# A decoder trunk on one core: the second FFN product in seven block products, with block sums made in DRAM

## The chip, the core and the metric

One core of a Trainium2 chip runs the whole program. TensorE (PE) multiplies into PSUM; VectorE (DVE), ScalarE (ACT) and GpSimd (POOL) work elementwise; SyncE's queue (SP) issues the loads and stores. The metric is the device time in microseconds of one execution: the median of three runs before the change is 1895.09 us (1895.04 to 1895.27).

## The reference

Two layers, each of three sub-layers with a residual and a layer norm: a token mixer (a gated recurrence beside windowed attention with learned sinks), cross-attention into 256 memory tokens, and a gated FFN. 512 tokens of width 1024, all float32. The change concerns the second product of the FFN, `... @ wo`, whose weight has 2816 rows and 1024 columns:

```python
D_FF = -(-8 * D_MODEL // (3 * 256)) * 256          # 2816

def swiglu(u, wi, wo):
    gate, up = jnp.split(u @ wi, 2, axis=-1)
    return (jax.nn.silu(gate) * up) @ wo

for l in range(DEPTH):                             # DEPTH = 2
    ...
    h = layer_norm(DEEPNORM_ALPHA * h + swiglu(h, ffn_wi[l], ffn_wo[l]), ln3_g[l], ln3_b[l])
```

and, of the attention, the maximum over the scores and the sink of each head:

```python
    sink = sinks.astype(jnp.float32).reshape(N_KV_HEADS, GROUP)[None, None, :, :, None, None]
    sink = jnp.broadcast_to(sink, scores.shape[:-1] + (1,))
    probs = jax.nn.softmax(jnp.concatenate([scores, sink], axis=-1), axis=-1)[..., :-1]
```

## The kernel before

Every float32 operand is split into a high part, rounded for fast multiplication, and a low part. A product of tiles is three matmuls: high by high, high by low, low by high. A weight comes as 128x1024 tiles of 512 KB. The class `Weights` keeps one list of them for the whole program, in order of use: `dma` loads the next into one of four `raw` buffers, on SP's queue; `split` makes the high part `whi` on ACT (L122) and the low part `wlo` on DVE (L123), and asks for further loads. `next` hands out a tile and splits `la` tiles ahead. The first product of the FFN and the query product of the cross-attention already work in seven block products (`split_quad`, `proj_pair`): there sums of weight blocks are made on DVE.

In the second product of the FFN, `out_norm` walks over the 22 row tiles of `wo`. For each row tile and each of four groups of 128 tokens it does six matmuls of 128x512 into two PSUM banks, so that eight banks hold the whole result; the activations `hs` are split by `h_parts` (ACT L271, DVE L272). The last five row tiles are taken group by group, and `norm` reads the residual x and the banks (L421, L435). Before these five, x is loaded back from `x_keep` in DRAM (L505).

The windowed attention (`swa_s`) works in 32 units a layer. A unit multiplies queries and keys, and builds the masked scores in a tile `sm` that has one more column for the sink. GpSimd copies the sink into that column (L603); ACT (L604) and DVE (L606) write the scores; DVE reduces the maximum over both (L608); the exponentials follow on ACT. There are six `sm` buffers. Before the change these 64 copies, some constants and six additions in the last norm are all that GpSimd has in its queue.

The code says which engine does what. A scheduler then orders the instructions of each engine, earlier code first among those that it reckons ready; each engine takes its queue in that order, and an instruction waits at its head on semaphores. The instructions of PE, DVE and ACT stand nearly as the code has them.

Of the kernel before, what the change touches and what calls it, by code (L numbers as in the profile page):

```python
# [7 lines left out]
F32 = mybir.dt.float32  # L8
# [37 lines left out]
class Weights:  # L46
# [27 lines left out]
    def rows(self, w, c0, n):  # L74
        for k in range(n):
            self.specs.append([(w[k * P:(k + 1) * P, c0:c0 + D], lambda t: t)])

    def gates(self, a, b):
        for n in range(4):
            self.specs.append([  # L80
                (m[n].rearrange("(k p) c -> p k c", p=P),
                 lambda t, i=i: t[:, i * 512:(i + 1) * 512].rearrange("p (k c) -> p k c", k=2))
                for i, m in enumerate((a, b))])
# [22 lines left out]
    def split(self):  # L106
        j = self.n_split
        if j >= len(self.specs):
            return
        while self.n_dma <= j:  # L110
            self.dma()
        if j in self.quad:
            self.drain()
            self.gen = self.split_quad(j)
            self.drain()
            return
        self.n_split += 1
# [95 lines left out]
class Trunk:  # L213
    def __init__(self, ctx, tc, a):
        self.tc = tc
        self.nc = tc.nc
        self.a = a
        self.L = a["w_in"].shape[0]
        pool = lambda name, bufs, **kw: ctx.enter_context(tc.tile_pool(name=name, bufs=bufs, **kw))
        self.const = pool("const", 1)  # L220
        self.pg = pool("pg", N_PAGES)
        self.raw = pool("raw", N_RAW)
        self.hpool = pool("hp", 8)
        self.smp = pool("sm", 3)
        self.sml = pool("sml", 8)
        self.psp = pool("ps", 8, space=PSUM)
        self.W = Weights(self)
        self.now = 0.0
        self.pend = []

    def page(self, dt=F32, name="pg"):
# [235 lines left out]
                nc.sync.dma_start(out=self.x_dram[t * P:(t + 1) * P, :], in_=xt)  # L467

    def out_norm(self, act, nk, res, gv, bv, last=False, prefetch=0, between=None,
                 want_T=False, restore=False, spread=0.0):  # L470

        nc = self.nc
        g = self.page(F32, "ln_g")
        nc.sync.dma_start(out=g, in_=gv.partition_broadcast(P))
        b = self.page(F32, "ln_b")
        nc.sync.dma_start(out=b, in_=bv.partition_broadcast(P))
        acc = [[self.ps("acc") for _ in range(2)] for _ in range(NT)]
        self.x_done = [False] * NT
        self.want_T, self.spread = want_T, spread
        self.Bf = {}  # L480

        cut = last

        def step(k, t, w, parts=((0, S), (S, D))):
            ah, al = act(k)
            hi, lo = w
            cs = slice(t * P, (t + 1) * P)
            kw = {"skip_group_check": True} if parts[0][1] - parts[0][0] < S else {}
            out = lambda c0, c1: acc[t][c0 // S][:, c0 % S:c0 % S + c1 - c0]
            for c0, c1 in parts:  # L490
                self.mm(out(c0, c1), ah[:, cs], hi[:, c0:c1], k == 0, False, **kw)
# [165 lines left out]
    def schedule_weights(self):  # L657
        a, W = self.a, self.W
        for l in range(self.L):
            wi = a["w_in"][l]  # L660
            XR, GR, QC, KV, GN, GA = 0, 1024, 2048, 3072, 3328, 4352
            W.cols(wi, KV, 1)
            W.cols(wi, QC, 1)
            W.cols(wi, KV + P, 1)
            W.cols(wi, QC + P, 1)
            W.cols(wi, GA, 1)
            for j in range(8):
                if j < 6:
# [12 lines left out]
            W.rows(a["ckv_w"][l], D, 8)  # L681
            for h in range(4):
                W.quads(a["cq_w"][l], 2 * h * P, (2 * h + 1) * P)
            W.rows(a["co_w"][l], 0, 8)
            for m in range(2):
                W.cols(a["ffn_wi"][l], m * P)
                W.cols(a["ffn_wi"][l], DFF + m * P)
            for m in range(2, NF):
                W.quads(a["ffn_wi"][l], m * P, DFF + m * P)
            W.rows(a["ffn_wo"][l], 0, NF)  # L690

    def layer_params(self, l):
        nc, a = self.nc, self.a
# [316 lines left out]
    def ffn(self, l, last):  # L1010
        nc, a, W = self.nc, self.a, self.W
        W.la = 0
        H, hs = {}, {}

        def act(m, g, u0, u1):
            s = self.half(name="silu")
            nc.scalar.activation(out=s, in_=g, func=AF.Silu)
            if m % 2 == 0:
                pg = self.page(F32, "h")
                H[m], H[m + 1] = pg[:, :S], pg[:, S:]  # L1020
            if u1 is None:
                nc.vector.tensor_tensor(out=H[m], in0=s, in1=u0, op=ALU.mult)
            else:
                nc.vector.tensor_tensor(out=H[m][:, :256], in0=s[:, :256], in1=u0, op=ALU.mult)
                nc.vector.tensor_tensor(out=H[m][:, 256:], in0=s[:, 256:], in1=u1, op=ALU.mult)

        def h_parts(k):
            for q in range(k, min(k + 3, NF)):
                if q in H:
                    t = self.page(F32R, "hs")  # L1030
                    self.split_to(t[:, :S], t[:, S:], H.pop(q), scale=1.0 / ALPHA)
                    hs[q] = t
            t = hs[k]
            if k - 1 in hs and k < NF - R3:
                hs.pop(k - 1)
            return t[:, :S], t[:, S:]

        p = self.proj_halves(4)
        act(0, p[0], p[1], None)
        act(1, p[2], p[3], None)  # L1040
        self.xt = [None] * NT
        for m in range(2, NF):
            act(m, *self.proj_pair())
        W.la = 2
        self.T = {}
# [27 lines left out]
    def run(self):  # L1073
        nc, a = self.nc, self.a
        self.xt = [self.page(F32, "x") for _ in range(NT)]
        self.mT_dram = [self.tc.dram_tile([P, 2, 2, MEM], F32, name="mT_keep%d" % i) for i in range(4)]
        self.x_dram = self.tc.dram_tile([S, D], F32, name="x_keep")
        self.xT = self.const.tile([P, ND, 2, S], F32R, name="xT")
        self.ident = self.const.tile([P, P], F32, name="ident")
# [76 lines left out]
```

## Time and profile before

| what | value |
|---|---|
| median of three runs | 1895.09 us |
| the profiled execution | 1894.67 us |
| its span, first to last instruction | 1892.8 us |
| PE busy | 1877.0 us, 99% |
| DVE busy | 1355.4 us, 72% |
| ACT busy | 1010.8 us, 53% |
| GpSimd busy | 27.5 us, 1% |
| moved by DMA | 217.63 MB |

The shares are means over stages of different kinds. The program runs the mixer, the cross-attention and the FFN of layer 0 until 945 us, and those of layer 1 after that. The granted clock of PE is 1.00 in the stages shown.

### The profile page before, as it was taken

What the parts mean: (1) busy time and instruction counts of PE and PEld (TensorE: products, weight loads), DVE (VectorE), ACT (ScalarE), POOL (GpSimd) and SP (SyncE); (2) the same over time, 40 slices, a digit from 0 to 9 for tenths busy, and PEclk for the clock granted to TensorE, in tenths of its full rate; (3) what the DMA queues carried; (4) which work ended last, traced back from release to release, by engine and by line L of the source; (5) the groups of instructions that cost most, each with busy time, mean ns of one, the idle gap of its engine ahead of it and who ended that gap; (6) DMA issues with size and microseconds to landing.
All of it is one profiled execution on the core that took longest, in us unless ns stands there. A gap on an engine that the chain in (4) does not pass through costs nothing.

```text
span 1892.8 us, 28893 instructions
## 1 busy us (share of the span) xinstructions
PE 1877.0 (99%) x11201; PEld 1666.6 (88%) x11201; DVE 1355.4 (72%) x2403; ACT 1010.8 (53%) x1973; POOL 27.5 (1%) x74
## 2 busy tenths in 40 slices
PE   9999999999999999999999999999999999999998
PEld 9888888889998999988898888888899899999886
DVE  6997367559766988873489964675588579888634
ACT  5675167336664655652346742763367556565521
POOL 0000000000000000000000000000000000000001
PEclk9999999999999999999999999999999999999999
DMA  6434133355444333364213441333652523333531
GB/s 183 112 101 121 47 100 90 100 167 191 122 142 127 90 112 101 101 191 144 67 46 104 109 123 44 101 95 95 200 178 80 181 75 112 101 107 107 188 100 45
DMA packets 277753, 217.63 MB, mean 115 GB/s; under 512 B 7792, under 2 KB 254064, under 8 KB 277616
## 3 DMA queue, kind: packets, MB, share of 16 engines
q1 hardware_dynamic: 277616, 215.79, 38.3%
q8 instruction: 88, 1.44, 0.3%
q14 instruction: 49, 0.40, 0.1%
HBM read 196.89 MB, written 12.58 MB: 111 GB/s over the span
## 4 chain that ended last, share of the span: by engine, by line
PE 96%; DVE 3%; ACT 1%; issue 0%; DVEq 0%; ACTq 0%
PE ps L244 40%; PE q L244 25%; PE acc L244 22%; PE cv L244 2%; PE sc L244 2%; PE av L244 1%; PE cs L244 1%; PE pt L248 1%; DVE Bf L346 1%; PE pT L248 1%; PE cT L248 0%; DVE wlo L123 0%; DVE xT L269 0%; DVE T1l L269 0%; PE scr L1062 0%
## 5 line engine op out<-in xcount | busy, mean ns | idle before, releaser
L244 PE MATMUL ps<-xT,whi 128*128 128x512 f32 (+1 forms) x1728 | 478.7, 365 | 1.2 <-ACT xT L268 0.7
L123 DVE TENSOR_TENSOR wlo<-raw,whi 128x1024 fp32r<-128x1024 f32 x239 | 290.4, 1222 | 142.2 <-ACT whi L122 114.0
L244 PEld LDWEIGHTS ps<-xT,whi 128*128 128x128 f32 x1728 | 297.4, 188 | 46.1 <-ACT xT L268 1.5
L122 ACT ACTIVATE whi<-raw 128x1024 fp32r<-128x1024 f32 x239 | 249.4, 1053 | 135.3 <-PE acc L244 52.4
L244 PE MATMUL ps<-xT,wlo 128*128 128x512 f32 (+1 forms) x864 | 310.8, 362 | 0.0
L244 PE MATMUL acc<-whi,hs 128*128 128x512 f32 (+1 forms) x714 | 218.3, 387 | 0.5 <-ACT hs L271 0.5
L244 PEld LDWEIGHTS ps<-xT,wlo 128*128 128x128 f32 x864 | 162.0, 188 | 27.6 <-DVE wlo L123 0.2
L244 PEld LDWEIGHTS acc<-whi,hs 128*128 128x128 f32 x714 | 133.5, 188 | 28.0 <-ACT hs L271 0.9
L244 PE MATMUL q<-xT,wq 128*128 128x256 f32 x1152 | 155.0, 281 | 0.1
L244 PEld LDWEIGHTS q<-xT,wq 128*128 128x128 f32 x1152 | 144.4, 189 | 0.6 <-DVE wq L269 0.5
L377 ACT ACTIVATE c<-q 128x256 f32<-128x256 f32 x192 | 73.5, 383 | 121.7 <-PE q L244 120.9
L244 PE MATMUL acc<-wlo,hs 128*128 128x512 f32 (+1 forms) x357 | 137.9, 386 | 0.0
L269 DVE TENSOR_TENSOR wql<-s,wqh 128x512 fp32r<-128x512 f32 x192 | 128.7, 684 | 1.4 <-ACT wqh L268 1.2
L268 ACT ACTIVATE wqh<-s 128x512 fp32r<-128x512 f32 x192 | 114.8, 622 | 15.2 <-DVE s L152 12.6
L269 DVE TENSOR_TENSOR wq<-raw,wq 128x512 fp32r<-128x512 f32 x144 | 98.4, 683 | 0.0
L268 ACT ACTIVATE wq<-raw 128x512 fp32r<-128x512 f32 x144 | 89.6, 622 | 3.3 <-DMA raw<-in_cq_w_dram 3.3
L244 PE MATMUL acc<-whi,mg 128*128 128x512 f32 x256 | 80.6, 392 | 0.0
L244 PE MATMUL acc<-whi,cO 128*128 128x512 f32 x256 | 80.2, 391 | 0.0
L244 PE MATMUL ps<-ya,whi 128*128 128x512 f32 x256 | 78.9, 389 | 0.0
L244 PEld LDWEIGHTS acc<-wlo,hs 128*128 128x128 f32 x357 | 67.0, 188 | 13.4
L244 PE MATMUL ps<-yr,whi 128*128 128x512 f32 x256 | 78.9, 389 | 0.0
L244 PE MATMUL q<-T4h,wq 128*128 128x256 f32 x384 | 76.7, 282 | 0.0
(237 smaller groups left out, 3968.3 us busy)
## 6 DMA issues: line engine op xcount, KB each, us to landing
raw<-in_ffn_wi_dram SPq DMA_DIRECT2D x88, 512.0 KB, 3.9
raw<-in_w_in_dram SPq DMA_DIRECT2D x84, 512.0 KB, 3.9
raw<-in_ffn_wo_dram SPq DMA_DIRECT2D x44, 512.0 KB, 4.2
raw<-in_ckv_w_dram SPq DMA_DIRECT2D x32, 512.0 KB, 4.5
raw<-in_w_br_attn_dram SPq DMA_DIRECT2D x16, 512.0 KB, 3.9
raw<-in_w_br_rnn_dram SPq DMA_DIRECT2D x16, 512.0 KB, 4.2
raw<-in_w_out_dram SPq DMA_DIRECT2D x16, 512.0 KB, 3.8
x_keep<-y SPq DMA_DIRECT2D x16, 512.0 KB, 2.6
```

The source lines that it names most:

```text
L122: nc.scalar.activation(out=hi, in_=raw, func=AF.Copy)
L123: nc.vector.tensor_sub(out=lo, in0=raw, in1=f(hi))
L244: self.nc.tensor.matmul(out, lhsT=lhsT, rhs=rhs, start=start, stop=stop, **kw)
L248: self.nc.tensor.transpose(out, in_, self.ident)
L268: nc.scalar.activation(out=hi, in_=src, func=AF.Copy)
L269: nc.vector.tensor_sub(out=lo, in0=src, in1=f(hi))
L346: nc.vector.tensor_tensor(out=o, in0=x, in1=y, op=ALU.subtract)
L377: cp = lambda out, in_: nc.scalar.activation(out=out, in_=in_, func=AF.Copy)
```

## The change

The first 2048 of the 2816 rows of `wo` are taken as two by two blocks of 1024 rows and 512 columns, B11, B12, B21 and B22, and the tokens as two halves of 256. The products of halves and blocks, eight of them, are replaced by seven products of sums. Every product has four tiles of 256 rows, and a tile twelve matmuls of 128x512.

The sums of weight blocks, `t[0]` = B11 + B12, `t[2]` = B12 + B22, `t[1]` = t[0] + B22 and `t[3]` = t[1] + B21, are made in DRAM by DMAs on GpSimd's queue: `block_sums` lists 32 of 256x512 for a layer, 16 that copy and 16 that add, and `split` takes one from that list each time. In layer 0 twelve empty entries stand ahead. The sums of activation blocks are made on DVE, in `operand`. Results of products that belong to more than one output block are added to x, or subtracted from it, by DVE out of PSUM (`into_x`); so x is now loaded ahead of the product. `out_norm` goes on in the same banks with the six row tiles that are left.

```diff
+    def blocks(self, w):
+        for j in range(4):
+            self.specs.append([(w[j * 256:(j + 1) * 256, :].rearrange("(k p) c -> p k c", p=P),
+                                lambda t: t.rearrange("p (k c) -> p k c", k=2))])
@@ def split(self):
         if j >= len(self.specs):
             return
+        if self.K.bg:
+            self.K.bg.pop(0)()
@@ def out_norm(..., acc=None, k0=0):
-        acc = [[self.ps("acc") for _ in range(2)] for _ in range(NT)]
+        fresh = [[acc is None or n is None for n in row] for row in acc] if acc else [[True] * 2] * NT
+        acc = [[acc[t][i] if not fresh[t][i] else self.ps("acc") for i in range(2)] for t in range(NT)]
-        for k in range(nk - res):
+        for k in range(k0, nk - res):
@@ def schedule_weights(self):
-            W.rows(a["ffn_wo"][l], 0, NF)
+            wo, t = a["ffn_wo"][l], self.wsum[l]
+            for b in (wo[0:D, 0:S], t[0], t[1], wo[D:2 * D, S:D], t[2], wo[D:2 * D, 0:S], t[3]):
+                W.blocks(b)
+            W.rows(wo[2 * D:DFF, :], 0, NF - 2 * ND)
+    def block_sums(self, l):
+        dma = self.nc.gpsimd.dma_start
+        wo, t = self.a["ffn_wo"][l], self.wsum[l]
+        B11, B12, B21, B22 = (wo[r * D:(r + 1) * D, c * S:(c + 1) * S] for r in range(2) for c in range(2))
+        seq = ((t[0], B11, 0), (t[2], B12, 0), (t[0], B12, 1), (t[2], B22, 1),
+               (t[1], t[0], 0), (t[1], B22, 1), (t[3], t[1], 0), (t[3], B21, 1))
+        for out, in_, add in seq:
+            for j in range(4):
+                r = slice(j * 256, (j + 1) * 256)
+                kw = {"accum_op": ALU.add} if add else {}
+                self.bg.append(lambda o=out[r, :], i=in_[r, :], kw=kw: dma(out=o, in_=i, **kw))
@@ def ffn(self, l, last):
+        W.la = 3
+        self.T = {}
+        self.xt = [self.page(F32, "x") for _ in range(NT)]
+        for t in range(NT):
+            nc.sync.dma_start(out=self.xt[t], in_=self.x_dram[t * P:(t + 1) * P, :])
+        acc = self.wo_seven(Hp)
...
         W.la = 2
         self.out_norm(h_parts, NF, R3, a["ln3_g"][l], a["ln3_b"][l], last=last,
-                      prefetch=0 if last else F3, restore=True)
+                      prefetch=0 if last else F3, acc=acc, k0=2 * ND)
+    def wo_seven(self, Hp):
+        ...
+        def product(p, b, first):
+            for j in range(4):
+                hi, lo = (t.rearrange("p (k c) -> p k c", k=2) for t in W.next())
+                i = p * 4 + j
+                while todo and todo[0][0] * 4 + todo[0][1] <= i + 2:
+                    operand(*todo.pop(0))
+                ah, al = ops.pop((p, j))
+                for k in range(2):
+                    for t in range(2):
+                        c = slice(t * P, (t + 1) * P)
+                        self.mm(b[t], ah[:, k, c], hi[:, k, :], first and j + k == 0, False, **kw)
+                        self.mm(b[t], ah[:, k, c], lo[:, k, :], False, False, **kw)
+                        self.mm(b[t], al[:, k, c], hi[:, k, :], False, j + k == 4, **kw)
+        def into_x(t0, hf, b, op):
+            for t in range(2):
+                x = self.xt[t0 + t][:, hf * S:(hf + 1) * S]
+                tt(out=x, in0=x, in1=b[t], op=op)
+        product(0, b1, True)
+        into_x(0, 0, b1, ALU.add)
+        product(1, b2, True)
+        into_x(2, 1, b2, ALU.add)
+        product(2, b1, False)
+        into_x(0, 1, b1, ALU.subtract)
+        product(3, b2, False)
+        product(4, b1, False)
+        into_x(2, 1, b1, ALU.subtract)
+        product(5, b3, True)
+        product(6, b1, False)
@@ def run(self):
         for l in range(self.L):
+            if l == 0:
+                self.bg = [lambda: None] * 12
+            self.block_sums(l)
             self.mixer(l, prm)
```

Two places show how the order of instructions changes. The first is GpSimd's queue at the start of the program. Before, the copies of the sink `sk` into the score tiles `sm` stand there, the first six of them with no other wait than that for the sink:

```order
L603 COPY sm<-sk 128x2 [waits DMAHW3_49]
L603 COPY sm<-sk 128x2 x5
L603 COPY sm<-sk 128x2 [waits DVE_49,PE_49,Pool_49] x2
L603 COPY sm<-sk 128x2 [waits PE_49,DVE_49,Activation_49,Pool_49] x6
L603 COPY sm<-sk 128x2 [waits DVE_49,PE_49,Pool_49]
```

Now the same queue begins as follows (`wsum_0_86` to `wsum_3_89` are the four sums of layer 0, `wsum_0_90` to `wsum_3_93` those of layer 1; rows that read alike are counted):

```order
L716 DMA wsum_0_86<-in_ffn_wo_dram 256x512 x4
L716 DMA wsum_2_88<-in_ffn_wo_dram 256x512 x4
L716 DMA wsum_0_86<-in_ffn_wo_dram 256x512 x4
L716 DMA wsum_2_88<-in_ffn_wo_dram 256x512 x4
L716 DMA wsum_1_87<-wsum_0_86 16x8192 x4
L716 DMA wsum_1_87<-in_ffn_wo_dram 256x512 x4
L716 DMA wsum_3_89<-wsum_1_87 16x8192 x4
L613 COPY sm<-sk 128x2 x6
L716 DMA wsum_3_89<-in_ffn_wo_dram 256x512 x4
L716 DMA wsum_0_90<-in_ffn_wo_dram 256x512 x4
L716 DMA wsum_2_92<-in_ffn_wo_dram 256x512 x4
```

28 transfers stand ahead of the first six copies. After these come the rest of layer 0's and, following one another, those of layer 1, up to the seventh copy, shown here with the semaphores that each waits for (DMASW0 to DMASW7 count the landings of GpSimd's transfers, eight in turn):

```order
L716 DMA wsum_3_93<-wsum_1_91 16x8192 [waits DMASW4_49]
L716 DMA wsum_3_93<-wsum_1_91 16x8192 [waits DMASW5_49]
L716 DMA wsum_3_93<-wsum_1_91 16x8192 [waits DMASW6_49]
L716 DMA wsum_3_93<-wsum_1_91 16x8192 [waits DMASW7_49]
L716 DMA wsum_3_93<-in_ffn_wo_dram 256x512 [waits DMASW0_49]
L716 DMA wsum_3_93<-in_ffn_wo_dram 256x512 [waits DMASW1_49]
L613 COPY sm<-sk 128x2 [waits DVE_49,PE_49,Pool_49]
```

62 of the 64 transfers stand ahead of the seventh copy. The rows of PE, DVE and ACT in the two mixers are those of before.

The second place is ACT's queue where the second product of the FFN begins in layer 0. Before, a weight split stands ahead of the silu, and the operand's splits right behind it:

```order
L377 ACTIVATE c_8677<-q_8674 128x256 [waits PE_49]
L122 ACTIVATE whi<-raw 128x1024 [waits DMAHW3_49,DVE_49]
L1017 ACTIVATE silu<-gt 128x512 [waits DVE_49]
L271 ACTIVATE hs<-h 128x512 x3
L122 ACTIVATE whi<-raw 128x1024 [waits DMAHW4_49]
```

Now the two weight splits stand between the silu and the first operand `hq`:

```order
L386 ACTIVATE c_8717<-q_8714 128x256 [waits PE_49]
L1043 ACTIVATE silu<-gt 128x512 [waits DVE_49,Activation_49]
L130 ACTIVATE whi<-raw 128x1024 [waits DMAHW3_49]
L130 ACTIVATE whi<-raw 128x1024 [waits DMAHW4_49]
L280 ACTIVATE hq<-h 128x512
```

The operand moved behind one weight split more, and the split that stood ahead of the silu moved behind it.

## Rows read from the trace of the kernel before

**Rows 1.** The page: the span, and busy us of each engine.

```profile
span 1892.8 us, 28893 instructions
...
PE 1877.0 (99%) x11201; PEld 1666.6 (88%) x11201; DVE 1355.4 (72%) x2403; ACT 1010.8 (53%) x1973; POOL 27.5 (1%) x74
```

**Rows 2.** Busy time by stretch: bounds, length, PE, PEld, DVE, ACT, POOL, clock, DMA share, GB/s.

```profile
60.00:100.00 40.00, 40.00 (x223) 34.25 (x223) 39.26 (x109) 26.59 (x78) 3.32 (x11) 1.00 0.35 92
...
826.00:945.00 119.00, 118.73 (x531) 98.26 (x530) 55.63 (x82) 42.87 (x63) 0.00 (x0) 1.00 0.42 129
```

**Rows 3.** Timeline of PE in the second product: start, us, engine, line, operation, count.

```profile
830.38 0.84 PE L244 MATMUL acc<-whi,hs 128*128 128x512 f32 x3
...
831.74 0.84 PE L244 MATMUL acc<-whi,hs 128*128 128x512 f32 x3
```

**Rows 4.** Groups by line and shape, 826 to 910 us: busy, mean ns.

```profile
L123 DVE TENSOR_TENSOR wlo<-raw,whi 128x1024 fp32r<-128x1024 f32 x23 | 28.1, 1223 | 36.6 <-ACT whi L122 21.5 <-issue 8.8 <-PE acc L244 6.4
L122 ACT ACTIVATE whi<-raw 128x1024 fp32r<-128x1024 f32 x22 | 23.0, 1053 | 32.4 <-PE acc L244 28.2 <-DVE hs L272 2.7 <-DMA raw<-in_ffn_wo_dram 1.5
L272 DVE SCALAR_TENSOR_TENSOR hs<-h,hs 128x512 fp32r<-128x512 f32 x19 | 12.9, 686 | 8.9 <-ACT hs L271 8.9
L271 ACT ACTIVATE hs<-h 128x512 fp32r<-128x512 f32 x19 | 11.6, 622 | 18.5 <-PE acc L244 18.5
```

**Rows 5.** Timeline of all engines at the entry of that product.

```profile
824.02 1.05 ACT L122 ACTIVATE whi<-raw 128x1024 fp32r<-128x1024 f32 x1
...
825.38 0.63 ACT L1017 ACTIVATE silu<-gt 128x512 f32<-128x512 f32 x1 [0.30 <-DVE gt L378]
...
825.91 1.66 ACT L271 ACTIVATE hs<-h 128x512 fp32r<-128x512 f32 x3
...
826.58 0.50 PE L244 MATMUL acc<-whi,hs 128*128 128x512 f32 x1 [0.27 <-ACT hs L271]
...
826.76 0.42 DVE L1025 TENSOR_TENSOR h<-silu,c 128x256 f32<-128x256 f32 x1
...
827.09 1.89 DVE L272 SCALAR_TENSOR_TENSOR hs<-h,hs 128x512 fp32r<-128x512 f32 x3
```

**Rows 6.** Timeline of GpSimd: the first seven sink copies.

```profile
21.73 1.80 POOL L603 COPY sm<-sk 128x2 f32<-128x2 f32 x6 [21.29 <-DMA sk<-in_sinks_dram]
49.23 0.29 POOL L603 COPY sm<-sk 128x2 f32<-128x2 f32 x1 [25.71 <-DVE qr L528]
```

**Rows 7.** Timeline of DVE: the first and seventh reduction, a weight split.

```profile
39.00 0.41 DVE L608 TENSOR_REDUCE nm<-sm 128x2 f32<-128x258 f32 x1
...
57.55 1.22 DVE L123 TENSOR_TENSOR wlo<-raw,whi 128x1024 fp32r<-128x1024 f32 x1
58.68 0.41 DVE L269 TENSOR_TENSOR PT<-pT,PT 128x256 fp32r<-128x256 f32 x1
...
60.70 0.42 DVE L608 TENSOR_REDUCE nm<-sm 128x2 f32<-128x258 f32 x1
```

**Rows 8.** Busy time by stretch at the program's start, columns as above.

```profile
0.00:20.00 20.00, 18.08 (x132) 17.55 (x133) 10.38 (x15) 9.74 (x14) 0.20 (x4) 1.00 0.93 274
...
0.00:39.00 39.00, 37.08 (x275) 35.74 (x276) 24.73 (x40) 17.23 (x25) 2.00 (x10) 1.00 0.75 209
...
0.00:65.60 65.60, 63.68 (x411) 57.85 (x412) 50.05 (x111) 34.40 (x79) 3.15 (x15) 1.00 0.59 165
```

**Rows 9.** DMA issues: count, KB each, median us from issue to landing.

```profile
raw<-in_w_in_dram SPq DMA_DIRECT2D x84, 512.0 KB, 3.9
...
x_keep<-y SPq DMA_DIRECT2D x16, 512.0 KB, 2.6
```

**Rows 10.** DMA queues: packets, MB, share of 16 engines' span.

```profile
q1 hardware_dynamic: 277616, 215.79, 38.3%
```

More of the change, by code (lines that the diff above doesn't have):

```diff
@@ L228, in __init__ @@
         self.now = 0.0
+        self.bg = []
         self.pend = []
@@ L469, in out_norm @@
     def out_norm(self, act, nk, res, gv, bv, last=False, prefetch=0, between=None,
-                 want_T=False, restore=False, spread=0.0):
+                 want_T=False, restore=False, spread=0.0, acc=None, k0=0):
         nc = self.nc
@@ L487, in step @@
             cs = slice(t * P, (t + 1) * P)
-            kw = {"skip_group_check": True} if parts[0][1] - parts[0][0] < S else {}
+            kw = {"skip_group_check": True} if k0 or parts[0][1] - parts[0][0] < S else {}
             out = lambda c0, c1: acc[t][c0 // S][:, c0 % S:c0 % S + c1 - c0]
             for c0, c1 in parts:
-                self.mm(out(c0, c1), ah[:, cs], hi[:, c0:c1], k == 0, False, **kw)
+                self.mm(out(c0, c1), ah[:, cs], hi[:, c0:c1], k == k0 and fresh[t][c0 // S], False, **kw)
                 self.mm(out(c0, c1), ah[:, cs], lo[:, c0:c1], False, False, **kw)
@@ L1012, in ffn @@
         W.la = 0
-        H, hs = {}, {}
+        H, Hp, hs = {}, {}, {}
         def act(m, g, u0, u1):
@@ L1018, in act @@
             if m % 2 == 0:
-                pg = self.page(F32, "h")
+                pg = Hp[m // 2] = self.page(F32, "h")
                 H[m], H[m + 1] = pg[:, :S], pg[:, S:]
@@ L1043, in ffn @@
             act(m, *self.proj_pair())
+        W.la = 3
[4 more added lines that the diff above has]
+        acc = self.wo_seven(Hp)
+        for m in range(2 * ND):
+            H.pop(m)
+        Hp.clear()
         W.la = 2
-        self.T = {}
         self.out_norm(h_parts, NF, R3, a["ln3_g"][l], a["ln3_b"][l], last=last,
-                      prefetch=0 if last else F3, restore=True)
+                      prefetch=0 if last else F3, acc=acc, k0=2 * ND)
@@ new lines, in wo_seven, with s, operand @@
+    def wo_seven(self, Hp):
+        nc, W = self.nc, self.W
+        tt = nc.vector.tensor_tensor
+        h = lambda j, tok: Hp[j].rearrange("p (k s) -> p k s", k=2)[:, :, tok * 256:(tok + 1) * 256]
+        st, ops = {}, {}
+        def s(j):
+            if j // 2 not in st:
+                st[j // 2] = self.page(F32, "hsum")
+            return st[j // 2][:, j % 2 * S:(j % 2 + 1) * S].rearrange("p (k s) -> p k s", k=2)
+        def operand(p, j):
+            if p in (0, 5):
+                src = h(j + (4 if p else 0), 0)
+            elif p == 6:
+                src = h(j + 4, 1)
+            elif p == 4:
+                src = h(j, 0)
+                tt(out=src, in0=src, in1=h(j, 1), op=ALU.subtract)
+            else:
+                src = s(j)
+                if p == 1:
+                    tt(out=src, in0=h(j, 1), in1=h(j + 4, 1), op=ALU.subtract)
+                elif p == 2:
+                    tt(out=src, in0=src, in1=h(j, 0), op=ALU.subtract)
+                else:
+                    tt(out=src, in0=src, in1=h(j + 4, 0), op=ALU.add)
+            t = self.page(F32R, "hq")
+            hi, lo = (t[:, i * S:(i + 1) * S].rearrange("p (k s) -> p k s", k=2) for i in range(2))
+            self.split_to(hi, lo, src, scale=1.0 / ALPHA)
+            ops[p, j] = hi, lo
+        todo = [(p, j) for p in range(7) for j in range(4)]
+        def product(p, b, first):
+            kw = {} if first else {"skip_group_check": True}
+            for j in range(4):
[10 more added lines that the diff above has]
+                        self.mm(b[t], al[:, k, c], hi[:, k, :], False, j + k == 4, **kw)
+                    self.tick()
+        def into_x(t0, hf, b, op):
+            for t in range(2):
+                x = self.xt[t0 + t][:, hf * S:(hf + 1) * S]
+                tt(out=x, in0=x, in1=b[t], op=op)
+        bank = lambda: [self.ps("acc") for _ in range(2)]
+        b1 = bank()
+        product(0, b1, True)
+        into_x(0, 0, b1, ALU.add)
+        b2 = bank()
+        product(1, b2, True)
[5 more added lines that the diff above has]
+        into_x(2, 1, b1, ALU.subtract)
+        b3 = bank()
+        product(5, b3, True)
+        product(6, b1, False)
+        return [[b3[0], b2[0]], [b3[1], b2[1]], [b1[0], None], [b1[1], None]]
@@ L1076, in run @@
         self.mT_dram = [self.tc.dram_tile([P, 2, 2, MEM], F32, name="mT_keep%d" % i) for i in range(4)]
+        self.wsum = [[self.tc.dram_tile([D, S], F32, name="wsum%d_%d" % (l, i)) for i in range(4)]
+                     for l in range(self.L)]
         self.x_dram = self.tc.dram_tile([S, D], F32, name="x_keep")
```

## The prediction

> **What bounds the kernel now.** I read the busy shares first: PE is busy 1877.0 of the span of 1892.8 us [rows 1], so a change gains what it takes off PE, unless another engine is made to keep PE waiting. The stages came next. PE is busy for 118.73 of the 119 us of the second FFN product of layer 0, and DVE is nearly idle there, 55.63 us. In the mixer it is the other way round: between 60 and 100 us PE is full and DVE is busy for 39.26 of 40 us [rows 2]. There DVE has no time to give, and whatever holds DVE holds PE a few us later. Then I read what stands in the queues that the change touches. GpSimd (Pool) does next to nothing: six tiny copies at 21.73 us, the seventh at 49.23 us, one for each unit of windowed attention [rows 6]. They are small but not free-standing: the max reduction of that unit on DVE (L608) waits for its copy, at 39.00 us for the first unit and at 60.70 us for the seventh [rows 7]. Last I read DMA: it is 93% busy in the first 20 us, and one queue, SP's, carries all the kernel's own transfers [rows 8, 10].
>
> **What the change takes away.** Sixteen row tiles of 24 matmuls become 28 block tiles of 12: 384 matmuls a layer become 336, all 128x512 as before. Six of them take from 830.38 to 831.74 us, so 0.227 us each [rows 3], and 96 in two layers are worth 21.8 us of an engine that is full there.
>
> **What it adds inside the FFN.** By layer, 12 more weight tiles to split, 12 more activation splits, 16 sums of activation blocks and 8 additions from PSUM into x. A split tile takes DVE 1.13 us from start to start (57.55 to 58.68) and an operation on 512 columns 0.60 us (three in 1.89 us, the last alone 0.69) [rows 5, 7]. For the 28 blocks DVE has 28 x (1.13 + 0.60) + 24 x 0.60 = 62.8 us to do; PE needs 336 x 0.227 = 76.2 us. ACT has 28 x (1.05 + 0.62) = 47 us [rows 4]. Both fit. Each addition into x waits for the end of a product, with one or two prepared block operands (2.7 us of PE each) in front of PE, and occupies DVE 1.2 us; its bank is used again one whole product later. I cost these waits at nothing; if that cover were gone, each of the eight pairs would show its 1.2 us, 10 us in all. The 28 blocks want 512 KB every 2.7 us, 193 GB/s, below the 274 GB/s of the first 20 us [rows 8]. The entry is dearer: ACT now has two weight splits between the silu and the first operand, where before one of them stood ahead of the silu and the other behind the operands (the second pair of order listings). The operand is ready at 825.91 + 2 x 1.05 + 0.62 = 828.6 instead of 826.5, and its low half on DVE at about 827.2 + 2 x 1.22 + 0.69 = 830.3, against a third matmul that would want it at 829.1 [rows 4, 5]. That is 2.1 + 1.2, about 3 us a layer, 6 us in all (bounds 0 and 12). The FFN alone so gains 21.8 - 6 = 16 us.
>
> **What it adds on Pool and DMA.** For each layer 32 transfers from DRAM to DRAM of 512 KB, half plain copies and half additions. They are popped one by one as weights are split, but Pool's order shows that this spacing does not survive: nothing but their own chain holds them. 28 stand ahead of the first sink copy, 62 ahead of the seventh, the 32 of layer 1 among them. Pool takes its queue in order, and each later transfer waits there for the one four or eight places ahead of it to land. The sixty-second waits for the landing of the fifty-eighth (third listing), so **the seventh copy can't run until 58 transfers are through**; DVE's reduction stands behind that copy, behind the reduction all of DVE's weight splits, and behind these PE.
>
> How long that takes no row shows, since no transfer of this kind is in the trace. From below: at the load rate, 274 GB/s at a busy share of 0.93, so 295 GB/s, 512 KB keep all engines busy for 1.78 us [rows 8]. A copy reads and writes DRAM, and an addition also reads what it adds to. Lower end: read and write overlap fully and the second read is free, one pass each, 58 x 1.78 = 103 us. Upper end: a copy costs two passes (3.56 us) and an addition three (5.34): 30 x 3.56 + 28 x 5.34 = 256 us. Neither end can be below nothing, since the bytes have to pass the same engines. The landing times of single loads and stores, 3.9 and 2.6 us [rows 9], lie inside both pairs of ends and hold a latency that transfers in flight share, so I take the middle: 2.67 and 4.45 us, 30 x 2.67 + 28 x 4.45 = 205 us. The loads up to that point take 0.59 x 65.6 = 39 us of the same engines [rows 8]. The seventh copy so comes at about 244 us (142 to 295), and DVE's seventh reduction, at 60.70 us before, is about **183 us late (81 to 234)**. The first copies are held too, behind 24 landed transfers: 12 x 2.67 + 12 x 4.45 = 85 us and 0.75 x 39 = 29 us of loads, so DVE's first reduction starts at about 115 us in place of 39.00. From there to the seventh it has 22 us of work, so this first wait lies within the larger one and isn't added. PE has a weight tile or so split ahead, which saves some 4 us. After the wait the transfers are done but for four, and layer 1 sees none.
>
> The Trainium skill has prices: "DMA: Bandwidth & Descriptors" (Latency and other measured facts) gives 214 GB/s for copies between DRAM tensors, and "Collectives: The Full Stack" (The bandwidth ceiling) says that a reducing transfer runs at about half the rate of a copying one, because it reads two sources. By these pages the 58 would take an estimated 30 x 2.45 + 28 x 4.9 = 211 us and the kernel 2063 us; no run here shows either rate yet.
>
> **The sum**, on the profiled execution's own 1894.67 us (its span is 1892.8 [rows 1], and 1.9 us lie around it; the median, 1895.09, is 0.02% above it): 1894.7 + 183 - 4 - 16 = **2057 us**. With the lower end 1894.7 + 81 - 4 - 16 = 1956; with the upper 2109, and if each of the 14 groups of four that wait for the group before it shows a whole landing of 3.9 us [rows 9], 55 us more: 2164.
>
> **The rivals.** *The transfers stay in the background*, as the code's spacing means them to: then only the FFN counts, 1894.7 - 16 = 1879 us, faster. It needs the 58 landings to come no more than 16 us after 60.70, by 77 us. With the loads' 39 us that leaves 38 us for 30 MB, 0.66 us each, which is 800 GB/s, against 295 GB/s as the best of a busy stretch. Against it speaks that number; for it, only that Pool might not hold its queue behind a waiting transfer, but the waits of the seventh copy behind a DVE instruction [rows 6] don't bear on this. 4 in 100, and 1 in 100 for ending near no change in between. *Pool is the slow one*: if it needs time of its own to issue a transfer, the chain is 58 times that, whatever the engines do. SP's loads land in 3.9 us, issue included [rows 9], but Pool has issued none. At 8 us each it gives 58 x 8 = 464 us, and 1894.7 + (464 - 61) - 20 = 2278 us; it decides from 244 / 58 = 4.2 us a transfer and passes 2170 from 6.1. 12 in 100 for all above 2170. *One pass each*: 1956 us; 7 in 100 for landing between 1899 and 1955.
>
> **How the numbers follow.** The forecast, a wait on Pool priced between one and three passes, has 76 in 100; the range is its bounds, 1955 to 2170, the upper one with landings between groups. Above it lie 12, below it 12 (7 slower, 1 the same, 4 faster). A difference of 0.2% (4 us) is about what can be told from none. Faster 0.04, the same 0.01, slower 0.95.
>
> **What would show it.** Right: Pool's first copies come near 115 us and its seventh near 244; DVE's longest waits are two for Pool's copies; the window from 60 to 240 us has PE nearly idle, the DMA busy and a second queue with 32 MB; after 300 us the stages have their old lengths; each FFN second product is about 8 us shorter (119 to 111), with 3 us of idle PE at its entry. Wrong: a seventh copy before 80 us; PE idle inside the seven products, behind DVE or loads; transfers that land in far under 1.8 us or far above 5 us each.

## The result, and the profile after

The changed kernel takes **1976.8 us** (median of 4 runs, 1975.8 to 1978.2) against 1895.1 us of the kernel before: a ratio of **1.043, interval 1.042 to 1.045**. It is slower, as forecast, and the time lies in the forecast's range of 1955 to 2170, but 80 us below its middle of 2057. Almost all of the loss is in the first 160 us. The page of after first: the span, busy us by engine, the span in 40 slices of 49.4 us, and the DMA queues.

```profile
span 1975.9 us, 29032 instructions
...
PE 1873.8 (95%) x11105; PEld 1661.4 (84%) x11105; DVE 1425.0 (72%) x2499; ACT 1047.0 (53%) x2021; POOL 74.2 (4%) x138
...
PE   4657999999999999999999999999999999999998
...
DMA  9997441333553523335642434133445252333571
...
q0 software_dynamic: 11520, 33.56, 7.0%
```

PE's matmuls fall from 11201 to 11105 as expected, and PE idles 102 us instead of 16 [rows 1]. Its busy time falls by only 3.2 us, though: in the run without transfers below, the same 11105 matmuls take 1861.4 us, 12.4 less, and the starved stretches shown next have granted clocks of 0.59 to 0.74. The first four slices hold most of the idle time, and in three of them the DMA is full. Queue q0 is new beside the one of [rows 10]: the 64 transfers. Their packets take 7.0% of 16 engines' span, 138 us, or 2.16 us a transfer. The same start by stretches, with the columns of [rows 8]:

```profile
20.00:40.00 20.00, 8.83 (x40) 8.34 (x41) 2.91 (x4) 2.80 (x4) 3.76 (x6) 0.59 1.10 234
40.00:60.00 20.00, 6.06 (x37) 5.56 (x36) 2.13 (x3) 1.54 (x2) 3.55 (x4) 0.67 1.08 279
60.00:80.00 20.00, 18.76 (x141) 17.39 (x140) 4.05 (x5) 4.15 (x5) 5.24 (x15) 0.97 1.00 269
80.00:100.00 20.00, 11.15 (x49) 9.49 (x50) 18.76 (x37) 11.63 (x25) 6.57 (x12) 0.74 1.08 260
100.00:120.00 20.00, 20.00 (x102) 16.41 (x102) 14.50 (x38) 9.38 (x32) 7.11 (x9) 1.00 1.07 245
120.00:140.00 20.00, 0.85 (x7) 0.64 (x5) 0.00 (x0) 0.00 (x0) 2.13 (x4) 0.65 1.09 277
140.00:160.00 20.00, 5.00 (x15) 3.98 (x15) 0.28 (x1) 0.00 (x0) 6.49 (x11) 0.59 1.05 263
...
180.00:200.00 20.00, 20.00 (x112) 17.20 (x111) 19.83 (x48) 13.94 (x42) 3.64 (x6) 1.00 0.33 86
```

From 20 to 160 us the DMA has no time left; packets overlap, so the share passes 1. Before, the stretch from 60 to 100 us took 0.35 [rows 2]. PE is starved twice for long, between 0 and 60 us and between 120 and 160, and for some 9 us between 80 and 100. The waits tell them apart. First the rows for ACT, then DVE, then PE, all from 0 to 170 us: who waits for whom, us in total, times, longest.

```profile
ACT sm L621 <- DVE nm L618: 52.5, 5, 46.0
ACT whi L130 <- DMA raw<-in_w_in_dram: 45.8, 6, 16.1
ACT whi L108 <- DMA raw<-in_w_in_dram: 11.4, 1, 11.4
```

```profile
DVE wlo L131 <- ACT whi L130: 45.2, 6, 16.5
DVE nm L618 <- POOL sm L613: 44.4, 1, 44.4
```

```profile
PE sc L253 <- DMA Q<-Qhl: 21.5, 1, 21.5
PE ps L253 <- ACT whi L130: 21.4, 3, 13.5
PE av L253 <- DVE PT L278: 14.5, 1, 14.5
```

The first starvation is loads: ACT can't split weights that haven't landed, and DVE and PE stand behind. The second holds the wait that the prediction named: DVE's max reduction stands 44.4 us behind a sink copy on Pool, and PE's 14.5 us for DVE's PT, up to 161.83 us, follow from it. But PE's 21.5 us just before, up to 142.31, are put down to another landing, that of the small transfers that lay out Q.

How late the loads come can be read directly. First SP's issue of one load of 256 KB, before and after (start, us); then the weight loads of the first 170 us, before and after (count, KB each, median us from issue to landing):

```profile
8.44 4.08 SPq L1097 DMA_DIRECT2D ropeC<-in_consts_dram  x1
25.95 26.15 SPq L1207 DMA_DIRECT2D ropeC<-in_consts_dram  x1
```

```profile
raw<-in_w_in_dram SPq DMA_DIRECT2D x22, 512.0 KB, 4.1
raw<-in_w_in_dram SPq DMA_DIRECT2D x15, 512.0 KB, 26.1
```

So the loads are late from SP on: SP stands 26 us in an issue that took 4 before, its next one starts at 52.14 us, and the weights land 26.1 us after their issue in the median, not 4.1. Pool's own rows and DVE's:

```profile
70.36 0.49 POOL L716 DMA_DIRECT2D wsum<-wsum  x1 [2.64 <-DMA wsum<-in_ffn_wo_dram]
...
76.76 0.78 POOL L613 COPY sm<-sk 128x2 f32<-128x2 f32 x6 [5.91 <-DMA sk<-in_sinks_dram]
...
159.16 0.52 POOL L613 COPY sm<-sk 128x2 f32<-128x2 f32 x1
```

```profile
93.56 0.41 DVE L618 TENSOR_REDUCE nm<-sm 128x2 f32<-128x258 f32 x1
...
159.72 0.42 DVE L618 TENSOR_REDUCE nm<-sm 128x2 f32<-128x258 f32 x1 [44.35 <-POOL sm L613]
```

The seventh reduction is 99.0 us later than in [rows 7]. From it to the end of the span before takes 1832.1 us (1892.8 - 60.70) and after 1816.2 (1975.9 - 159.72), 15.9 less. So +99 and -16 make the 83 us between the two spans.

### The profile page after: what moved, and what is told of

The parts are those of the page before. It is cut to its first block, busy times and chain, and to the rows that moved or that the text cites. A ratio compares the mean times of both kernels' runs of the same rounds, so it can differ in the third digit from the quotient of the medians.

```text
span 1975.9 us, 29032 instructions
## 1 busy us (share of the span) xinstructions
PE 1873.8 (95%) x11105; PEld 1661.4 (84%) x11105; DVE 1425.0 (72%) x2499; ACT 1047.0 (53%) x2021; POOL 74.2 (4%) x138
## 3 DMA queue, kind: packets, MB, share of 16 engines
q0 software_dynamic: 11520, 33.56, 7.0%
## 4 chain that ended last, share of the span: by engine, by line
PE 86%; DMA 5%; DVE 4%; SPq 3%; ACT 1%; issue 1%; POOL 0%; DVEq 0%; POOLq 0%; ACTq 0%
PE ps L253 35%; PE q L253 24%; PE acc L253 20%; DMA wsum<-in_ffn_wo_dram 3%; PE av L253 1%; SPq L1207 1%; PE sc L253 1%; PE cs L253 1%; PE cv L253 1%; SPq L1200 1%; DVE Bf L355 1%; DMA upper<-in_consts_dram 1%; DVE wlo L131 1%; PE pt L257 1%; PE pT L257 1%
## 5 line engine op out<-in xcount | busy, mean ns | idle before, releaser
L253 PE MATMUL ps<-xT,whi 128*128 128x512 f32 (+1 forms) x1728 | 486.4, 370 | 33.2 <-ACT whi L130 21.4
L131 DVE TENSOR_TENSOR wlo<-raw,whi 128x1024 fp32r<-128x1024 f32 x263 | 319.3, 1222 | 117.4 <-ACT whi L130 115.1
L253 PEld LDWEIGHTS ps<-xT,whi 128*128 128x128 f32 x1728 | 303.2, 192 | 79.2 <-ACT whi L130 22.0
L130 ACT ACTIVATE whi<-raw 128x1024 fp32r<-128x1024 f32 x263 | 274.3, 1052 | 120.5 <-DMA raw<-in_w_in_dram 50.2
L253 PE MATMUL acc<-whi,hq 128*128 128x512 f32 x448 | 140.8, 395 | 5.6 <-ACT hq L280 4.4
L253 PEld LDWEIGHTS acc<-whi,hq 128*128 128x128 f32 x448 | 85.2, 191 | 24.9 <-ACT hq L280 4.8
L621 ACT ACTIVATE sm<-sm,nm 128x129 f32<-128x129 f32 x128 | 50.5, 397 | 77.2 <-DVE nm L618 76.9
L253 PE MATMUL acc<-wlo,hq 128*128 128x512 f32 x224 | 88.1, 393 | 0.0
```

The costliest lines, as they stand in the source:

```text
L253: self.nc.tensor.matmul(out, lhsT=lhsT, rhs=rhs, start=start, stop=stop, **kw)
L621: nc.scalar.activation(out=sm[:, e, :P + 1], in_=sm[:, e, :P + 1], func=AF.Exp, bias=nm[:, e:e + 1], accum_out=es[:, e:e + 1])
```

## The experiments

Two accounts stood against each other. **A**, the prediction's: the queue on Pool is the cause, because the sink copy stands behind the transfers. **B**: the transfers take DMA time from the loads of the first 160 us, and the wait on Pool only stands where a wait for loads would stand. The first four runs separate the parts and these two. In the recorded expectations the letters A, B and C stand for what each text says there, which is not always the same.

**No transfers.** The blocks of the weight itself stand where the sums stood, and the sums are left out.

```
-  for b in (wo[0:D, 0:S], t[0], t[1], wo[D:2 * D, S:D], t[2], ...
+  for b in (wo[0:D, 0:S], wo[0:D, S:D], wo[0:D, S:D], wo[D:2 * D, S:D], ...
-  self.block_sums(l)
```

> The seven products with no transfer on GpSimd: where a sum of weight blocks would be read, a block of the weight itself is read, so the sums are left out and the numbers that come out are not the reference's. Theory A (all of the loss comes from the transfers at the start, and the FFN gains what the blind sum said): 1895 - 16 = 1879 us, 1876 to 1882; the changed kernel's stretch from DVE's seventh reduction to the end was 1816.2 us against 1832.1 before, 15.9 shorter. Theory C (part of the 82 us is lost in the FFN or after it): above 1885 us, with PE idle inside the seven products.

Measured: **1881.45 us** (1880.84 to 1884.08), ratio 0.993, interval 0.991 to 0.994. The seven products alone are faster, by 13.65 us.

**Transfers alone.** The kernel before with `block_sums` and its 64 transfers added; nobody reads the sums.

```
+  if self.K.bg:
+      self.K.bg.pop(0)()          # behind each split
...
+  if l == 0:
+      self.bg = [lambda: None] * 12
+  self.block_sums(l)
```

> The kernel before with the 64 transfers on GpSimd as the change has them, their results unused. Theory A: the seventh reduction is 99 us late as in the changed kernel and nothing is gained in the FFN: 1895 + 98 = 1993 us, 1988 to 1998. Theory C: 1977 us or less.

Measured: **1990.2 us** (1988.6 to 1990.5), ratio 1.050, interval 1.049 to 1.052. The two parts add up: 1895.1 + 95.1 - 13.65 = 1976.6, against 1976.8 for the whole change. The 95 us are the transfers' alone.

**Sink copies on ACT.** One line of the changed kernel; no sink copy stands behind a transfer any more.

```
-  nc.gpsimd.tensor_copy(out=sm[:, :, P], in_=self.sink[...])
+  nc.scalar.activation(out=sm[:, :, P], in_=self.sink[...], func=AF.Copy)
```

> The changed kernel with the sink copies on ACT in place of GpSimd, so that no copy stands behind a transfer. Theory A (two causes: loads that come late, 54 us by DVE's first reduction, and GpSimd's queue, 44 us at the seventh): the 44 us go, 1977 - 44 = 1933 us, 1920 to 1945, and 32 more small instructions a layer on ACT cost under 6 us. Theory B (the transfers take the loads' bandwidth until they are done, and the wait on GpSimd only stands where a wait for loads would stand): 1970 to 1980 us, with DVE or ACT waiting for loads between 115 and 160 us.

Measured: **1975.1 us** (1972.9 to 1977.4), ratio 1.042, interval 1.041 to 1.044. Taking the hold on Pool away gains nothing that can be told from zero, so the hold is not needed for the loss. In this trace, from 0 to 170 us, no wait of DVE on Pool is left and the wait for loads has grown from 45.8 to 70.7 us (ACT's row); PE's rows show that it is starved all the same:

```profile
ACT whi L130 <- DMA raw<-in_w_in_dram: 70.7, 8, 15.1
```

```profile
PE sc L253 <- DMA Q<-Qhl: 22.4, 2, 21.1
PE ps L253 <- ACT whi L130: 19.2, 3, 12.0
PE sc L253 <- DVE Q L281: 17.0, 1, 17.0
```

The seventh reduction starts at 140.52, 19 us earlier than in after, but the ninth at 163.17, since the weights, and the small transfers from SBUF to SBUF that lay out Q, come no sooner. DMA is at 1.04 to 1.11 in every stretch from 20 to 160 us here too.

**Copies only.** Each addition becomes a plain copy of the same bytes, so the sums are left out.

```
-  kw = {"accum_op": ALU.add} if add else {}
+  kw = {}
```

> The changed kernel with its 32 adding transfers made plain copies, so the sums are left out. It prices an addition against a copy. If an addition costs about twice a copy (landings 3.1 us apart against 1.3 to 1.7 in the changed kernel's start): 58 transfers at 1.4 us are 81 us, the seventh sink copy comes near 115 us instead of 159, DVE arrives there about then, and the time is 1977 - 44 = 1933 us or some 20 less, as the loads find more room: 1910 to 1935. If an addition costs what a copy does: 1970 to 1980 us.

Measured: **1946.9 us** (1943.7 to 1949.6), ratio 1.027, interval 1.026 to 1.029; between the two expected ranges, and in neither. Its queue, and its seventh reduction:

```profile
q0 software_dynamic: 7424, 33.56, 5.0%
```

```profile
130.04 0.42 DVE L618 TENSOR_REDUCE nm<-sm 128x2 f32<-128x258 f32 x1 [26.23 <-POOL sm L613]
```

5.0% of the span of 1947.8 us is 97.4 us for 64 copies, **1.52 us a copy**. In after 138.3 us are 32 copies and 32 additions, so **an addition takes 2.80 us**, 1.84 times a copy. With these two the prediction's own sum comes out: 30 x 1.52 + 28 x 2.80 + 39 us of loads = 163 us for the seventh copy (measured 159.16), and 58 x 1.52 + 39 = 127 us here, where the reduction behind it starts at 130.04.

What was open then was whether the transfers cost their time wherever they lie. The next three runs move them.

**Paced, behind the attention units.** Each transfer waits for a tiny gate: ACT copies two columns of a landed weight tile, and a DMA of 1 KB on Pool ties them to the transfer's target. No transfer starts before some 30 splits.

```
-  self.bg.append(lambda o=out[r, :], i=in_[r, :], kw=kw: dma(out=o, in_=i, **kw))
+  def one(o=out[r, :], i=in_[r, :], kw=kw, raw=None):
+      g = self.small(2, "rs")
+      self.nc.scalar.activation(out=g, in_=raw[:, 0:2], func=AF.Copy)
+      if kw:
+          dma(out=g, in_=o[0:128, 0:2])
+      else:
+          dma(out=o[0:128, 0:2], in_=g)
+      dma(out=o, in_=i, **kw)
+  self.bg.append(one)
...
+  self.bg = [lambda raw: None] * (34 if l == 0 else 30)
```

> The same 64 transfers, but each is let go only when a weight tile behind the attention units has been split: ACT copies two columns of that tile into a small tile, and a tiny DMA on Pool with it stands ahead of each transfer. Layer 0's 32 start behind 34 splits, layer 1's are let go in layer 1 behind 30. Theory B (the delay of the change is DMA time that the loads of the first 160 us don't get; the seventh sink copy's wait on Pool only ends at the same time): with the transfers where the DMA is 30 to 40% busy the delay goes, 1895 - 14 = 1881 us, as without any transfers (1881.45), up to 1890 if loads land later beside them. Theory C (64 transfers cost their time wherever they lie, because an accumulating DRAM write slows the loads beside it): 1910 to 1960. Wait on Pool alone (theory A): 1881 too, since no sink copy stands behind a transfer in the first units; it is told apart from B by the run with the sink copies on ACT, not here.

Measured: **1893.8 us** (1886.7 to 1904.8), ratio 1.000, interval 0.998 to 1.001. It is just above the 1881 to 1890 expected of B, and far from the 1910 of C. 83 of the 95 us are gone; 12 remain above the run without transfers, and the times scatter more. ACT's timeline in the recurrent branch (start, us, operation, idle before it) shows one such place:

```profile
276.05 0.20 ACT L718 ACTIVATE rs<-raw 128x2 f32<-128x2 f32 x1 [1.76 <-DMA raw<-in_w_in_dram]
276.27 1.28 ACT L856 ACT_TABLE_LOAD   x1
...
281.89 1.07 ACT L128 ACTIVATE whi<-raw 128x1024 fp32r<-128x1024 f32 x1
```

The gate (L718) was put ahead of the split it belongs to: it holds ACT until a load has landed that ACT needs almost 6 us later. In all of this trace ACT sat idle 92 us ahead of such gates, in 35 waits for loads. So I took the 12 us for the gate's price, not the transfers'; the run in the first FFN product, below, moves the transfers and changes the gate at once, so the two are not separated.

**The same, with two early operands.** The first two activation operands of the seven products are split before the last pair of the first FFN product, not behind it.

```
-  for m in range(2, NF):
+  for m in range(2, NF - 1):
       act(m, *self.proj_pair())
+  self.early(Hp)                  # operands (0, 0) and (0, 1)
+  act(NF - 1, *self.proj_pair())
...
```

> The paced transfers, and in each layer the first two activation operands of the FFN product are split ahead of the last pair of the first FFN product instead of behind it. The prediction held the entry of the product to be 3 us of idle PE a layer dearer, 6 in all. If that is so, this runs about 6 us under the paced version, 1875 us (1872 to 1879); if the entry's idle time moves elsewhere (the first product then waits for the third operand, or the last pair is put back by the two splits on ACT and DVE), within 2 us of it.

Measured: **1885.5 us** (1878.2 to 1893.5), ratio 0.995, interval 0.992 to 0.997: 8.3 us under the run above, at the same scatter. The time expected, 1872 to 1879, took the paced version to be at 1881; the step expected was 6 us. The two waits for these operands, 6.0 us in all, are gone from PE's list.

**Layer 0's transfers at the start, layer 1's paced.** As the paced version, with layer 0's 32 transfers issued without gates behind 12 splits, as in the change.

```
+  def one(...):
+      if l == 0:
+          dma(out=o, in_=i, **kw)
+          return
...
+  self.bg = [lambda raw: None] * (12 if l == 0 else 30)
...
```

> Layer 0's 32 transfers at the start as in the change, layer 1's 32 paced in layer 1. The chain of the first 32 ends at about 80 us in place of 160. Theory B (bandwidth: the delay is the time of the transfers that lie ahead of the attention units): about half of the 95 us of the 64, 1881 + 40 to 55 = 1921 to 1936 us. Theory A (the wait of the seventh sink copy): its queue then holds 28 to 30 of 32 landings ahead of the seventh copy, until about 75 us in place of 61, so some 15 us: 1896 us (1890 to 1905).

Measured: **1948.4 us** (1945.0 to 1949.6), ratio 1.028, interval 1.027 to 1.029. Account A's 1896 is out, and B's 1921 to 1936 is too low: the first 32 transfers cost more than half. Pool's seventh copy and DVE's seventh reduction:

```profile
106.42 0.52 POOL L613 COPY sm<-sk 128x2 f32<-128x2 f32 x1 [25.20 <-DVE sm L616]
```

```profile
117.32 0.42 DVE L618 TENSOR_REDUCE nm<-sm 128x2 f32<-128x258 f32 x1
```

The reduction is 56.6 us late, and its copy waited for a DVE instruction, not for a transfer. The first unit's reduction is at 94.00, as in after (93.56). So the first 32 transfers put back the start, where PE waits for loads as they land, by 57 us; the other 32 of the change add 42. What makes these cheaper, no run shows.

The last three test what is left: is it the place or the burst, and was the gate the 12 us?

**In the first FFN product.** A layer's transfers are let go during its own first FFN product (600 to 825 us in layer 0), one behind each half of a pair of weight tiles, and the gate reads the split tile, ACT's own output. The early operands are kept.

```
+  o["A11"] = one(a1)
+  if K.bg:
+      K.bg.pop(0)(f(o["A11"][0]))
...
+  o["A12"] = one(a2)
+  if K.bg:
+      K.bg.pop(0)(f(o["A12"][0]))
...
-  self.nc.scalar.activation(out=g, in_=raw[:, 0:2], func=AF.Copy)
+  self.nc.scalar.activation(out=g, in_=hi[:, 0:2], func=AF.Copy)
...
```

> As the paced version with the two early operands, but each layer's 32 transfers are let go in that layer's first FFN product, one behind every half of a pair of weight tiles, and the gate's two columns are copied from the split tile (ACT's own output) and not from the landed load. The paced versions lost 12 us in the recurrent branch of the mixer, where ACT stood before the gate waiting for a load. Theory B with that read of the loss (the 12 us are the gate's place on ACT, and transfers in a stretch with 30 to 40% busy DMA cost nothing): 1881.45 - 6 for the entry = 1875.5 us, 1873 to 1879. Theory C (the transfers themselves cost 12 us beside any loads): 1885 to 1890.

Measured: **1874.6 us** (1873.7 to 1875.5), ratio **0.989, interval 0.988 to 0.991**. It does the whole computation, with the same 64 transfers, and beats both kernels.

**No transfers, with the early operands.** The floor for the one above. In place of the sums the products read other blocks than in the first run without transfers, of the same size.

> No transfers at all (the products read blocks of the weight where the sums would stand, so the sums are left out) and the two early operands. The floor that the seven products can reach here: 1881.45 us less the entry's idle time of 2.2 + 0.7 us a layer in the trace without transfers, 1875.6 us (1874 to 1878). If taking the entry's idle time away only moves it behind the next operand: 1880 to 1882.

Measured: **1873.3 us** (1873.1 to 1873.7), ratio 0.989, interval 0.987 to 0.990, 0.7 us below the expected range. The 64 transfers in their new place cost 1.3 us, within what the runs can tell.

**A burst in the same place.** Only a layer's first eight copies have gates; the other 24 follow as fast as they can.

```
+  def one(hi, n=len(self.bg), ...):
+      if n < 8:
+          ...                      # the gate
+      dma(out=o, in_=i, **kw)
+      if n == 7:
+          while self.bg:
+              self.bg.pop(0)(None)
```

> As the version with the transfers in the first FFN product, but only the first eight copies of a layer are let go by gates; the other 24 follow as fast as their own chain lets them: a burst of 32, as at the start, but in a stretch where the loads keep the DMA 30 to 37% busy and stand four tiles ahead. Theory B with the starting point as what decides (at the start PE waits for every load, DMA 93% busy): nothing or a few us, 1875 to 1880. Theory B with the burst as what decides (loads starve beside 4 to 8 transfers in flight wherever they are): the burst of some 75 us starves the loads as at the start, where 32 cost 61 us: 1875 + 2 x 30 to 60 = 1935 to 1995.

Measured: **1932.2 us** (1926.4 to 1937.1), ratio 1.020, interval 1.017 to 1.022: 57.5 us above the paced one, 29 for each burst of 32 (1932 is just under the 1935 expected of the burst as the cause). Rows of both traces between 660 and 720 us, paced first, then the burst (bounds, length, PE, PEld, DVE, ACT, POOL, granted clock, DMA share, GB/s):

```profile
660.00:680.00 20.00, 20.00 (x170) 20.00 (x169) 17.25 (x33) 11.83 (x29) 5.15 (x8) 1.00 0.84 204
680.00:700.00 20.00, 20.00 (x170) 20.00 (x169) 17.25 (x33) 11.83 (x29) 5.55 (x8) 1.00 0.99 204
```

```profile
660.00:680.00 20.00, 13.17 (x108) 12.76 (x107) 11.63 (x22) 7.76 (x18) 6.82 (x10) 0.91 1.07 293
...
700.00:720.00 20.00, 12.42 (x90) 12.22 (x89) 8.61 (x16) 5.84 (x13) 2.01 (x3) 0.83 1.09 234
```

And DVE's wait for landing weights there: in the paced run from 620 to 780 us, in the burst from 620 to 720 us, with PE's wait of the same 100 us below it.

```profile
DVE s L157 <- DMA raw<-in_ffn_wi_dram: 1.1, 1, 1.1
```

```profile
DVE s L157 <- DMA raw<-in_ffn_wi_dram: 19.8, 5, 7.9
...
PE q L255 <- ACT c L388: 16.0, 6, 7.6
```

Paced, PE is full at a DMA share of up to 0.99. In the burst the share is 1.07 to 1.10 from 640 to 720 us, the loads come up to 7.9 us too late, PE stands 16 us for what is behind them, and the granted clock falls to a mean of 0.91 and 0.83, part of the stretch at 1.2 GHz instead of 2.4. SP's four loads ahead are no cover there.

## Why the prediction was right, and where it was off

**Direction and range: right.** The transfers come in a burst at the start, not spread as the code spaces them; the gain in the FFN is small beside that. The rival "in the background" (1879 us) needed 58 landings by 77 us; Pool issued its twenty-eighth transfer, which waits for the twenty-fourth to land, at 70.36 us. The version paced in the FFN achieves what that rival meant, by another order. Of the signs named for being right, the second queue came, with 33.56 MB. The long idle times of PE lie before 60 us and from 120 to 160, not from 60 to 240, and DVE had one long wait for Pool, not two.

**The 21.8 us of PE time: right.** The run without transfers or entry wait is 21.8 us under the kernel before (1895.1 - 1873.3), as forecast from 96 x 0.227. That the digits agree is luck: in the two profiled executions PE's busy time falls by 20.7 us, from 1877.0 [rows 1] to

```profile
PE 1856.3 (99%) x11105; PEld 1647.9 (88%) x11105; DVE 1423.9 (76%) x2499; ACT 1045.6 (56%) x2021; POOL 27.4 (1%) x74
```

**The entry: right in kind, too small.** Forecast 3 us a layer; PE's rows in the seven products of layer 1 of after show it, and no other gap there:

```profile
PE acc L253 <- ACT hq L280: 2.2, 1, 2.2
PE acc L253 <- DVE hq L281: 0.8, 1, 0.8
```

But early operands gain 8.1 us (1881.45 - 1873.3), not 6. What the traces show beside the gap is the clock. In the run without transfers, the stretch behind the gap of layer 0 has PE full at a mean granted clock of 0.71, between its levels of 1.2 and 2.4 GHz; with early operands it is at 2.4 throughout, 1.00. Each row is the ten microseconds from 830 us, first without and then with early operands:

```profile
830.00:840.00 10.00, 9.95 (x32) 7.95 (x33) 9.03 (x12) 5.08 (x7) 0.00 (x0) 0.71 0.71 219
```

```profile
830.00:840.00 10.00, 10.00 (x45) 8.13 (x45) 7.60 (x11) 4.28 (x6) 0.00 (x0) 1.00 0.71 262
```

32 matmuls fill the first row, 45 the second. The execution traced took 1884.08 us, more than the median, so the clock's part in the median's 8.1 us is not measured. With the entry at 8.1 instead of 6 the forecast's 16 us for the FFN become 13.7; that this is the 13.65 measured is no check, since both come from the same three medians. The 15.9 us from the seventh reduction on hold this and some 2 us of the slack of PE, which was taken as 4.

**The additions into x, DVE's and ACT's budgets in the seven products: right.** PE has no wait inside them. DVE, called nearly idle in that product before the change, was busy for 55.63 of 119 us [rows 2]; its sum of 62.8 us did not depend on that word.

**The price of a transfer: the term that was mis-sized.** 2.67 and 4.45 us were the middle of the bounds; 1.52 and 2.80 us were measured, so the 58 transfers took 124 us and not 205. The range was wide enough to hold this. The copy lies below the lower bound of 1.78 us, which was taken from a rate of loads: these transfers between DRAM tensors moved their bytes faster than loads into SBUF did in the kernel before. With the measured prices the same sum, loads included, gives 163 us for the seventh copy in place of 244, a delay of some 102 us (99.0 measured), and with the measured one 1894.7 + 99 - 4 - 13.7 = 1976 us. The loads' 39 us, which the sum added to the chain, were needed: without them the seventh copy would come at 124. The estimate by the pages of the Trainium skill erred the same way. In the Trainium skill, "DMA: Bandwidth & Descriptors" (Latency and other measured facts) has 214 GB/s for copies of other tiles between DRAM tensors, issued on other queues; this case shows 345 (512 KB in 1.52 us of all engines), and the measurement decides. In the Trainium skill, "Collectives: The Full Stack" (The bandwidth ceiling) has a reducing transfer of a collective at about half the rate; 2.80 against 1.52 us, a factor of 1.84, agrees roughly.

**The mechanism: half right.** The hold on Pool is there in the trace, 44.4 us, and it is the last wait on the path. But the loss does not need it: with the sink copies on ACT the time is the same, since the loads of the same stretch are late by as much. Whether the hold alone, beside loads that come on time, would have cost as much is not shown. What the sum priced was right for another reason: it added up DMA time, and DMA time is what ends both waits. The step "DVE's reduction stands behind that copy", taken as the way into PE, was one of two ways.

**The first wait: wrong.** Pool's first copies were put at 115 us behind 24 landings; they came at 76.76 us. The measured prices would have put them at 12 x 1.52 + 12 x 2.80 + 29 = 81, but the wait that ended last was the one for the load of the sinks. DVE's first reduction, at 93.56, waited for neither: DVE came to it late, behind weights that had landed late. This is the step that was wrong: the prediction saw loads only as time added to the chain, never as what the chain pushes aside; the windows of before at 0.93 busy [rows 8] said that there was nothing to push into.

**Pool as a slow issuer: out.** A transfer takes Pool 0.5 to 0.9 us to issue, 0.49 in the row at 70.36, and the landings set the pace: there Pool stood 2.64 us for one.

What stays open: how the engines share out time between the two queues, why SP's issue is held, and how much of the paced version's 12 us was the gate. The burst in the FFN and the one at the start differ by a factor of two in price (29 and 57 us for 32 transfers); that the start has no loads ahead of use, and so pays more, is argued from the waits, not separated by a run.

## What to carry to other kernels

Price a background transfer by the DMA time it takes, against what its stretch has left, and look at how many stand in flight beside the loads: 64 transfers cost 95 us in a burst at the start, 57 in two bursts later, and 1.3 when each waits for a piece of compute in a stretch with room. When a queue's hold and a full DMA show at the same place, removing the hold tells whether the loss needs it; the last wait on the path need not be it. Here the spacing of DMA issues that the code meant was lost, and it came back once a dependency enforced it.

## What the runs showed of the hardware that I had not expected

- A copy of 512 KB between DRAM tensors took 1.52 us of the 16 engines, less than a load of the same size at the best rate of before (1.78 us); an accumulating one took 2.80 us. It has more packets as well: (11520 - 7424) / 32 = 128 more than a copy's 116.
- Beside 4 to 8 such transfers in flight, a weight load landed a median of 26.1 us after issue, against 4.1 before, and SP stood 26.15 us in one issue; the paced transfers, at a DMA share of 0.75 to 0.99 between 640 and 780 us, in layer 0's first FFN product, left PE no wait there, and all 64 cost 1.3 us.
- Three microseconds of idle PE at the entry of a product were followed, in one trace, by ten at a mean granted clock of 0.71. Taking the gaps of both layers away gained 8.1 us, 4 us for each gap of 3.
